# A sixth buffer of split weights and a fourth of raw weights, in room taken from the dynamic DMA scratch

## The chip, the cores and the metric

The kernel runs on one core of a Trainium2 chip, as one launch. The metric is the device time of that launch in microseconds, as the median of several runs. The engines are TensorE (PE in the profile; PEld its weight loads), VectorE (DVE), ScalarE (ACT), GpSimd (POOL) and SyncE (SP), each with an instruction stream of its own.

## The reference, cut to what matters

One inference step of a small backbone of two trunk layers, in fp32, over 640 tokens (512 latent tokens of a 2-D grid and 128 context tokens) of 1024 channels:

```
every layer: x += 1/2 * gate1 * SwiGLU1(mod(rmsnorm(x)))
             x += gate2 * Mixer_l(mod(rmsnorm(x)))
             x += 1/2 * gate3 * SwiGLU2(mod(rmsnorm(x)))
layer 0:     Mixer = w_in -> [2-D neighbourhood attention | bidirectional RG-LRU] -> w_out_ab
layer 1:     Mixer = real part of the 2-D DFT of the normalised input, then w_out_c
mod(h)     = h * (1 + scale) + shift;  shift, scale, gate from SiLU(cond) @ w_ada[l] + b_ada[l]
swiglu(h)  = (silu(h @ w_gate) * (h @ w_up)) @ w_down
```

So there are four FFNs, two mixers, and the products for the modulation vectors (w_ada). Outputs are the tokens, new context keys and values, and the last states of the RG-LRU.

## The kernel before

**Layout.** x is kept transposed (channels on partitions), as two halves of 320 tokens. A product in fp32 is made of three passes of a shorter format: with each operand split into a high and a low part, it adds high·high, high·low and low·high (`mm3`, L271).

**Weights.** They come from HBM as *units* of 128x1024 numbers. SP issues the load (`load`, L129) into a *raw* buffer (tile `st`, 4 KB of each partition). ACT makes the high part (`whi`, L176), and DVE the low part (`wlo`, L181, subtracting the high part from the raw weights), into a *pair* (`whi` and `wlo` together, 8 KB of each partition). In the program `split_later` (L174) emits ACT's instruction and leaves DVE's to `flush` (L179), which comes at the head of the next `prep`. During the attention POOL makes the low parts.

The kernel has 3 raw buffers and 5 pairs for its whole length (L51). A phase adds its own: each FFN adds 3 raw buffers, the attention 1 pair and 4 raw buffers, and the opening 5 raw buffers.

**The order of the work** is written out by the Python program: each engine runs its instructions in the order in which they were emitted, and the semaphores between the engines are put in from the tiles used. `prep(upto, most)` (L151) is called between the matmuls. It emits the next steps of weight preparation, in a fixed list, as long as their item's number lies under `upto`, a raw buffer has been filled by a load, and a pair is free. Then `load` issues the loads for which raw buffers are free. `done()` frees the oldest unit's pair and calls `prep(n_use + LS)`, with LS = 4 units ahead of the one in use. So the number of buffers and the two limits together decide at which place of DVE's and ACT's streams a split is put.

**FFN.** The inner width is cut into chunks. The first two take 4 units (gate and up of two chunks), which run chunk by chunk while the norm of the input is made (`mm_side`, L285, `ffn_body`, L726; the first FFN of all has `ffn_start`). Beside them runs the norm of half 1, `norm_steps`, whose first three steps are emitted together (`step(3)`, after the fifth of the eight chunks of half 0). Ahead of them come the sums `nst`, the reciprocal root on DVE (a chain of eleven instructions on 128x3 numbers, `nv`, `ns` and `nt`, L415 to L422) and the factors `dg`, which PE spreads over the partitions (`nbc`, L453). The chunks after that are *quads*: gate and up of a chunk, each in two halves, form a 2x2 matrix, for which the Strassen–Winograd scheme needs 7 products in place of 8. A quad has two raw units and makes three pairs from them: `A1`, `S24` and `S3` (plus a single-part buffer, `S1`). Its steps are `quad_a` (split of A1), `quad_b` and `quad_c` (two sums each on POOL, L226 to L232, in place in the raw buffers), `quad_f` (split of S24), `quad_d` (split of S1, tile `s`) and `quad_e` (split of S3, which frees the second raw buffer). `quad_c` overwrites the raw unit that `A1` was split from, and so it waits for that `wlo`; the split of S24 reads what `quad_c` makes. In a quad the products are matmuls into `q`; the products of the first two chunks go to `pg`, and those with w_down to `pd`.

**In time** (from the profile): FFN 1 of layer 0 is 0 to 500 us, mixer 0 is 500 to 838 (attention about 690 to 778), then FFN 2 of layer 0 to 1300, FFN 1 of layer 1 to 1745, the Fourier mixer to 1850, and FFN 2 of layer 1 to the end. Text and rows call the last three of the FFNs' beginnings the second, third and fourth *entry*.

**Small loads.** Two constants, `pk` (192 KB) and `pk2` (27 KB), hold the biases and the norm's weights. POOL issues their loads at the start (L1619, L1621); they are the only transfers on its queue. All weights are loaded by SP.

Of the kernel before, what the change touches and what calls it, by code (L numbers as in the profile page):

```python
# [13 lines left out]
PSUM = bass.MemoryType.PSUM  # L14
# [18 lines left out]
class Item:  # L33
    """weights of one product: their loads, the steps that split them, what the steps made"""
# [7 lines left out]
class Kern:  # L42
    def __init__(self, ctx, nc, tc, a):
        self.ctx, self.nc, self.tc, self.a = ctx, nc, tc, a
        pool = lambda name, bufs, **k: ctx.enter_context(tc.tile_pool(name=name, bufs=bufs, **k))
        self.const = pool("const", 1)
        self.t2 = pool("t2", 2)
        self.ps2 = pool("ps2", 2, space=PSUM)
        self.ps_st, self.ps_pairs = ctx.enter_context(ExitStack()), None
        self.st_free, self.w_free = [], []  # L50
        self.buffers(self.const, None, 3, 5)  # L51
        self.loads, self.steps, self.items, self.used = [], [], [], []
        self.n_use = 0
        self.LS = 4
        self.limit = 9999
        self.lows, self.b12, self.t_todo, self.nst = [], {}, [], {}
        self.add_eng = None
        self.T_ENG = [nc.gpsimd if x == "p" else nc.vector for x in TE]
        self.s_dma = self.s_use = 0
        self.slab_t = {}  # L60
        self.ada_m = None
        self.low = nc.vector

    def buffers(self, pool, phase, n_st, n_w):
        """buffers for weights: as loaded, and split; those of a phase serve its weights only"""
        for j in range(n_st):
            self.st_free.append((pool.tile([P, 1024], F32, name=f"st{j}"), phase))
        for j in range(n_w):
            self.w_free.append((pool.tile([P, 1024], F32R, name=f"whi{j}"),
                                pool.tile([P, 1024], F32R, name=f"wlo{j}"), phase))  # L70
# [14 lines left out]
    def slab_pool(self, st, upto, bufs=2):  # L85
        """weights of the adaLN vectors: slabs up to this one are used in the phase"""
        self.slab_p = st.enter_context(self.tc.tile_pool(name="slab", bufs=bufs))
        self.s_dma = self.s_use
        self.s_end, self.s_bufs = upto, bufs

    def psum(self, pairs):
        """PSUM of a phase: six single banks or three pairs"""
        if self.ps_pairs is pairs:
            return
        self.ps_st.close()
        self.ps_pairs = pairs
        ps = self.ps_st.enter_context(self.tc.tile_pool(name="ps", bufs=3 if pairs else 6, space=PSUM))
        if pairs:
            self.pair = lambda name: ps.tile([P, 2, 512], F32, tag="mm", name=name)
            self.bank = lambda name: self.pair(name)[:, 0, :]  # L100
        else:
            self.bank = lambda name: ps.tile([P, 512], F32, tag="mm", name=name)
# [48 lines left out]
    def prep(self, upto, most=99):  # L151
        """steps for the items up to this one, as far as there are buffers"""
# [21 lines left out]
    def split_later(self, it, hi, lo, src, then=None):  # L174
        """the low part comes with the next step"""
# [20 lines left out]
    def fold_a(self, it, w):  # L196
        """rows m and -m: sum and difference"""
# [12 lines left out]
    # a pair of units as a 2 x 2 matrix (unit, half of the rows): the seven left factors of Strassen and Winograd  # L210
# [59 lines left out]
    def done(self, most=99):  # L270
        """the oldest unit in use is no longer needed"""  # L271
        self.free_slot(self.used.pop(0), 0)
        self.prep(self.n_use + self.LS, most)

    def mm3(self, out, w, ks, xs, first=True, last=True):
        """out (+)= W^T X in three passes; w: (hi, lo) as [P, k, 128], xs: k -> (hi, lo)"""
# [8 lines left out]
    def mm_side(self, outs, ws, h, lag=0):  # L285
        """products of several units with half h, chunk after chunk as the norm gives them; the last two unit by unit
        lag: chunks by which the last unit stays behind"""
# [57 lines left out]
    def ada_end(self):  # L345
        """the finished vector, channels on partitions"""
# [28 lines left out]
    def parts(self, h):  # L375
        """pieces of a token half with one condition: (column slice, condition)"""
# [20 lines left out]
    def norm_s(self, h, bank=None):  # L397
        """sums of squares, tokens on partitions"""
# [6 lines left out]
    def norm_a(self, h):  # L405
        """rsqrt(mean(x^2) + eps)"""
# [4 lines left out]
    def rsqrt(self, ps, n=3):  # L411
        """rsqrt(mean(x^2) + eps) of n columns of sums"""
# [3 lines left out]
        # the exponent halved on the bits, then Newton's steps  # L416
# [21 lines left out]
    def T_pool(self, ks=range(4)):  # L438
        """right factors of Strassen and Winograd beside the parts of h"""
# [9 lines left out]
    def norm_r(self):  # L449
        """the factors of the tokens on all partitions"""  # L450
# [6 lines left out]
    def norm_high(self, h, l, i, c, r, keep):  # L457
        """h = rms_norm(x) g (1 + scale) + shift and its high part
        keep: for the products of a SwiGLU"""
# [24 lines left out]
    def direct(self, l, i, h, c, keep):  # L484
        """the high part comes without the sum of product and shift"""
# [19 lines left out]
    def norm_steps(self, h, l, i, keep=False):  # L505
        """a step for each chunk, low parts one step behind"""
# [17 lines left out]
    def t_sums(self, k, b12, b22):  # L524
        """T1 = B12 - B11, T2 = B22 - T1, T3 = B22 - B12, T4 = B21 - T2"""
# [21 lines left out]
    # slabs of a SwiGLU: after chunks of the first units, and after each quad  # L547
# [5 lines left out]
    def plan_ffn(self, l, n, s):  # L553
        """weights of a SwiGLU in the order of their use; s: the first slab, returns the next"""
# [36 lines left out]
    def ffn(self, l, i, after, mid=iter(()), late=None):  # L591
        """after(h, c): what follows the last update of chunk c, half h; mid: steps of other work, one in each quad;
        late: what follows the last quad"""
# [14 lines left out]
    def ffn_start(self, evac):  # L608
        """the first products of all: the first two vectors of adaLN come chunk by chunk, the norm and the products follow"""
# [7 lines left out]
        def ada(c):  # L617
            """the vectors' values for a chunk, four sums in groups of columns"""
# [178 lines left out]
    def down_last(self, fs, gate, after):  # L797
        """the last product before a norm: half 0 is through while four chunks of half 1 remain
        the first sums wait for the last chunk of the inner width"""
# [20 lines left out]
    def quad(self, f, fills, begin=False):  # L820
        """gate and up of a chunk, both halves of the tokens, in seven products
        M1 = A11 B11, M2 = A12 B21, M3 = S4 B22, M4 = A22 T4, M5 = S1 T1, M6 = S2 T2, M7 = S3 T3;
        C11 = M1 + M2, U2 = M1 + M6, C12 = U2 + M5 + M3, C21 = U2 + M7 + M4, C22 = U2 + M7 + M5"""
# [73 lines left out]
    def out_last(self, xs, gate, after):  # L897
        """the last product before a norm: half 0 is through while four chunks of half 1 remain"""
# [32 lines left out]
    def mix_setup(self):  # L931
        """parameters of the mixer, log_sigmoid(lambda)"""
# [13 lines left out]
        # y = |lam|, w = exp(-y) by halving steps and a series  # L946
# [17 lines left out]
        # log1p(w) = 2 artanh(w / (2 + w))  # L964
# [11 lines left out]
        # -2 log_sigmoid = 2 (2 artanh) - 2 min(lam, 0)  # L976
# [24 lines left out]
    def lru(self, c, xc, gel):  # L1001
# [21 lines left out]
        for d in range(2):  # L1023
            # exp(-z) and t = tanh(z / 2): 1 - a = t (1 + a), 1 - a^2 = t (1 + a)^2
# [28 lines left out]
    def qk_norm(self, which, c, ps):  # L1053
        """RMS norm over each head's 64 channels; q also gets -1/8"""
# [47 lines left out]
    def mixer0(self, after):  # L1102
        nc, tc = self.nc, self.tc
        self.bg, self.fg = [], []
        with ExitStack() as st:
# [18 lines left out]
            with ExitStack() as s2:  # L1124
# [60 lines left out]
                def early():  # L1185
                    """work that the first tiles of the attention cover"""
# [41 lines left out]
    def bias(self, c, v):  # L1228
        """mask less position bias of a variant of the windows' columns"""
# [122 lines left out]
    def fourier_const(self):  # L1352
        """the DFT matrices in the place of the right factors, a step for each piece"""
# [18 lines left out]
        def steps():  # L1372
# [9 lines left out]
            # the shift times the root of the number of tokens, by chunk in the group, group, condition  # L1382
# [10 lines left out]
    def scaled(self, h, c):  # L1393
        """x g (1 + scale) in parts; the factors of the tokens follow the channels' transform"""
# [12 lines left out]
    def fourier_front(self, const):  # L1407
        """what follows the updates before the transform"""
# [25 lines left out]
    def tok_rest(self):  # L1434
        """factors of the other tokens; the third tile has the end of half 0 and the start of half 1"""
# [8 lines left out]
    def fourier(self, after):  # L1444
        nc, tc = self.nc, self.tc
        NP, NQ, MP, MQ = self.NP, self.NQ, self.MP, self.MQ
        with ExitStack() as st:
# [6 lines left out]
            with ExitStack() as s2:  # L1454
# [11 lines left out]
                def chan(k, g):  # L1466
                    """the channels' transform: token tile k, group g"""
# [9 lines left out]
                def chan_out(k, g):  # L1477
                    """times the factors of the tokens, in parts"""
# [26 lines left out]
                # the shift's part, the same for all tokens  # L1505
# [25 lines left out]
                def pos(r):  # L1531
                    """rows r: cosines of group r, 4 the Nyquist channels, 5 + g sines of group g"""
# [9 lines left out]
                    def shift(q):  # L1542
                        """the shift stays at the first position"""
# [18 lines left out]
            with ExitStack() as s2:  # L1562
# [14 lines left out]
                for c in range(KD):  # L1577
# [17 lines left out]
                    # token n has the sum, the one as far from the end the difference  # L1595
# [16 lines left out]
    def run(self, stop=99):  # L1612
        nc, a = self.nc, self.a
        const = self.const
        with self.tc.manual_schedule():
# [3 lines left out]
            nc.gpsimd.dma_start(out=pk, in_=a["pk"])  # L1619
            self.pk2 = const.tile([P, 54], F32, name="pk2")  # L1620
            nc.gpsimd.dma_start(out=self.pk2, in_=a["pk2"])  # L1621
# [48 lines left out]
            def after(l, i, first=4, per=3, keep=True):  # L1670
                """the next norm: half 0 while the last products of half 1 run"""
# [49 lines left out]
def pack(inp):  # L1721
    """lays the inputs out; no arithmetic"""
# [9 lines left out]
    # the first two vectors by chunks of channels  # L1732
# [47 lines left out]
    # DFT matrices: channels (columns: cosines 0..127, the first halved, cosine 128, sines 1..127) and positions  # L1780
# [37 lines left out]
```

## Time and profile before

| | |
|---|---|
| device time, three runs | 2305.51, 2307.77, 2308.82 us (median 2307.77) |
| span of the profiled execution | 2305.0 us |
| instructions | 39901 |
| PE busy | 2224.0 us (96%), 15534 matmuls |
| DVE, ACT, POOL busy | 1554.8, 990.7, 954.9 us |
| HBM | 245.44 MB moved, 105 GB/s |

The span runs from the first to the last instruction of one execution, and is the profiled execution's own time; no other time is given for it. A timeline row gives the start and the duration of an instruction (or of several alike in a row, "x2"), what it writes and reads, and in brackets how long its engine had been idle and which instruction, of which engine and line, ended that. "us" in the table of stretches is busy time per engine, and the number between 0 and 1 after the engines is TensorE's granted clock as a share of 2.4 GHz.

### The profile page before, as it was taken

The page shows a single profiled execution, that of the slowest core. Times are in us where ns is not written, and L with a number is a line of the kernel's source. Part 1 is how long each engine was busy: PE and PEld are TensorE (multiplying, and loading weights), DVE is VectorE, ACT ScalarE, POOL GpSimd, SP SyncE. Part 2 cuts the span into 40 slices and gives each one's busy share as a digit, 9 for nine tenths or more (in the row PEclk, how much of TensorE's full clock was granted, in tenths as well). Part 3 has the DMA queues.
Part 4 walks back from the last instruction along what each step waited for, and adds up shares of the span by engine and source line. Part 5 has one row for each costly group of instructions (what it writes and reads, how often), then busy time and mean ns, then how long its engine had stood idle before and what let it go on. Part 6 is the DMA issues. An engine that isn't in the chain of part 4 may idle for free.

```text
span 2305.0 us, 39901 instructions
## 1 busy us (share of the span) xinstructions
PE 2224.0 (96%) x15534; PEld 2110.0 (92%) x15534; DVE 1554.8 (67%) x2871; ACT 990.7 (43%) x1780; POOL 954.9 (41%) x856
## 2 busy tenths in 40 slices
PE   7999999999998899999999999999999989999999
PEld 5889999999994788999999889999999979999999
DVE  6676677666865368666666786666667786666665
ACT  4433333347855435333333453333335553333332
POOL 2444444440023235444444454444443645444441
PEclk9999999999999999999999999999999999999999
DMA  7333333321228424333322243332332322222221
GB/s 278 113 111 105 105 107 107 115 74 56 73 71 267 131 83 137 110 101 110 106 91 97 75 155 120 110 97 96 103 117 62 128 85 83 83 83 83 83 89 57
DMA packets 75316, 245.44 MB, mean 106 GB/s; under 512 B 8756, under 2 KB 12996, under 8 KB 75128
## 3 DMA queue, kind: packets, MB, share of 16 engines
q1 hardware_dynamic: 74168, 241.28, 31.7%
q8 instruction: 123, 2.02, 0.4%
q10 hardware_dynamic: 864, 1.38, 0.2%
q14 instruction: 65, 0.53, 0.1%
q0 software_dynamic: 96, 0.22, 0.0%
HBM read 239.71 MB, written 3.15 MB: 105 GB/s over the span
## 4 chain that ended last, share of the span: by engine, by line
PE 79%; DVE 13%; ACT 4%; issue 2%; POOL 2%; DMA 1%; ACTq 0%; DVEq 0%; SPq 0%; POOLq 0%
PE q L282 40%; PE pd L282 26%; PE pj L282 5%; DVE wlo L181 2%; PE ada L327 2%; DVE tl L172 1%; PE pg L282 1%; PE gt L1014 1%; PE pos L1549 1%; DVE x L381 1%; PE S L1262 1%; DVE y L473 1%; DVE sx L1268 1%; PE PT L1288 1%; DMA st<-w_ada 1%
## 5 line engine op out<-in xcount | busy, mean ns | idle before, releaser
L181 DVE TENSOR_TENSOR wlo<-st,whi 128x1024 fp32r<-128x1024 f32 (+2 forms) x401 | 498.4, 1254 | 11.1 <-ACT whi L176 10.2
L176 ACT ACTIVATE whi<-st 128x1024 fp32r<-128x1024 f32 (+2 forms) x405 | 401.2, 992 | 233.0 <-POOL st L232 139.3
L282 PE MATMUL pd<-g,whi 128*128 128x320 f32 x1536 | 347.0, 310 | 4.3 <-DVE u L825 2.3
L381 DVE SCALAR_TENSOR_TENSOR x<-pd,mods,x 128x128 f32<-128x128 f32 (+2 forms) x696 | 265.0, 433 | 111.7 <-PE pd L282 111.2
L282 PE MATMUL q<-hh,wlo 128*128 128x320 f32 x960 | 296.9, 309 | 5.3 <-DVE wlo L181 5.3
L282 PE MATMUL q<-hh,whi 128*128 128x320 f32 x960 | 300.7, 313 | 1.0 <-DVE u L825 1.0
L282 PE MATMUL q<-th,whi 128*128 128x320 f32 x960 | 297.3, 310 | 3.0 <-DVE sg L825 3.0
L282 PE MATMUL q<-tl,whi 128*128 128x320 f32 x960 | 296.6, 309 | 0.7 <-POOL tl L172 0.7
L282 PE MATMUL q<-th,wlo 128*128 128x320 f32 x960 | 296.6, 309 | 0.0
L282 PE MATMUL q<-hl,whi 128*128 128x320 f32 x960 | 296.3, 309 | 0.0
L231 POOL TENSOR_TENSOR st<-sums,st 128x512 f32<-128x512 f32 x80 | 118.0, 1474 | 396.9 <-DVE wlo L181 359.5
L825 POOL TENSOR_TENSOR u<-u,u 128x320 f32<-128x320 f32 x80 | 106.5, 1331 | 401.0 <-DVE u L825 401.0
L282 PEld LDWEIGHTS pd<-g,whi 128*128 128x128 f32 x1536 | 256.8, 188 | 8.9 <-DVE x L381 3.1
L282 PE MATMUL pd<-hh,whi 128*128 128x320 f32 x768 | 238.4, 310 | 0.0
L282 PE MATMUL pd<-hl,whi 128*128 128x320 f32 x768 | 237.9, 310 | 0.0
L282 PE MATMUL pd<-g,wlo 128*128 128x320 f32 x768 | 237.7, 310 | 0.0
L282 PE MATMUL pd<-hh,wlo 128*128 128x320 f32 x768 | 236.8, 308 | 0.0
L826 ACT ACTIVATE sg<-sg 128x320 f32<-128x320 f32 x160 | 75.4, 471 | 284.5 <-DVE sg L825 284.5
L282 PEld LDWEIGHTS q<-hh,whi 128*128 128x128 f32 x960 | 180.2, 188 | 16.8 <-issue 8.6
L282 PEld LDWEIGHTS q<-th,whi 128*128 128x128 f32 x960 | 180.3, 188 | 6.6 <-issue 4.7
L282 PEld LDWEIGHTS q<-hh,wlo 128*128 128x128 f32 x960 | 180.2, 188 | 6.4 <-DVE wlo L181 6.4
L282 PEld LDWEIGHTS q<-tl,whi 128*128 128x128 f32 x960 | 180.4, 188 | 1.5 <-POOL tl L172 1.5
(327 smaller groups left out, 5016.0 us busy)
## 6 DMA issues: line engine op xcount, KB each, us to landing
st<-w_ada SPq DMA_DIRECT2D x144, 512.0 KB, 4.6
st<-ffn_gate SPq DMA_DIRECT2D x88, 512.0 KB, 3.6
st<-ffn_up SPq DMA_DIRECT2D x88, 512.0 KB, 3.7
st<-ffn_down SPq DMA_DIRECT2D x96, 384.0 KB, 3.1
st<-w_in SPq DMA_DIRECT2D x20, 512.0 KB, 3.5
st<-ffn_down SPq DMA_DIRECT2D x16, 512.0 KB, 3.5
st<-w_out_ab SPq DMA_DIRECT2D x8, 512.0 KB, 3.5
st<-w_out_c SPq DMA_DIRECT2D x8, 512.0 KB, 3.5
```

Of the source, the lines that this page charges most:

```text
L172: (eng or self.nc.vector).tensor_tensor(out=lo, in0=src, in1=hi.bitcast(F32), op=ALU.subtract)
L176: self.nc.scalar.activation(out=hi, in_=src, func=AF.Copy)
L181: self.low.tensor_tensor(out=lo, in0=src, in1=hi.bitcast(F32), op=ALU.subtract)
L231: self.nc.gpsimd.tensor_tensor(out=s[:, 0:512], in0=it.s1, in1=s[:, 0:512], op=ALU.subtract)
L282: self.nc.tensor.matmul(out, lhsT=l, rhs=r, start=first and j == 0, stop=last and j == len(ops) - 1)
L327: nc.tensor.matmul(self.ada_ps[32 * j:32 * j + 32, 0:256], lhsT=self.s_sb[:, k, :], rhs=t[:, 256 * j:256 * j + 256], start=k == 0, stop=k ...
L381: self.nc.vector.scalar_tensor_tensor(out=self.x[h][c][:, sl], in0=ps[:, sl], scalar=gate[:, c, r:r + 1], in1=self.x[h][c][:, sl], op0=ALU ...
L473: nc.vector.tensor_tensor(out=y, in0=self.x[h][c], in1=r, op=ALU.mult)
L825: tt = lambda e, o, a, b, op=ALU.add: e.tensor_tensor(out=o, in0=a, in1=b, op=op)
L826: cp = lambda o, p, fn=AF.Copy: nc.scalar.activation(out=o, in_=p, func=fn)
L1014: nc.tensor.matmul(g[:, s, 0:322], lhsT=wt[:, d, j, :], rhs=xc[:, 322 * s:322 * s + 322], start=True, stop=True)
L1262: nc.tensor.matmul(o, lhsT=q, rhs=k, start=True, stop=True)
```

## The change

The pool of dynamic DMA scratch of the program is set to 1024 bytes. The two small loads are issued by ScalarE, in front of its first activation, in place of GpSimd. In the room, `buffers` gets 4 raw buffers and 6 pairs in place of 3 and 5 for the kernel's whole length: 4 KB and 8 KB of each partition. No limit of `prep` and no order of steps is changed. The other lines of the diff take out comments and docstrings and leave the line numbers as they were.

```
@@ Kern.__init__ @@
-        self.buffers(self.const, None, 3, 5)
+        self.buffers(self.const, None, 4, 6)
...
@@ Kern.run @@
-            nc.gpsimd.dma_start(out=pk, in_=a["pk"])
+            nc.scalar.dma_start(out=pk, in_=a["pk"])
             self.pk2 = const.tile([P, 54], F32, name="pk2")
-            nc.gpsimd.dma_start(out=self.pk2, in_=a["pk2"])
+            nc.scalar.dma_start(out=self.pk2, in_=a["pk2"])
...
@@ kernel @@
-    nc = _bacc.Bacc("TRN2", target_bir_lowering=False, num_devices=1)
+    nc = _bacc.Bacc("TRN2", target_bir_lowering=False, num_devices=1, dynamic_dma_scratch_size=1024)
```

## Rows read from the trace of the kernel before

**Rows 1.** The page: busy us of each engine (share) x instructions.

```profile
PE 2224.0 (96%) x15534; PEld 2110.0 (92%) x15534; DVE 1554.8 (67%) x2871; ACT 990.7 (43%) x1780; POOL 954.9 (41%) x856
```

**Rows 2.** Stretches: start:end, length, busy us by engine, granted clock, DMA share, GB/s.

```profile
510.00:520.00 10.00, 7.45 (x45) 7.22 (x43) 7.97 (x17) 5.60 (x11) 7.87 (x26) 0.83 0.28 98
850.00:860.00 10.00, 7.48 (x30) 7.17 (x31) 6.35 (x18) 3.47 (x7) 3.12 (x4) 0.66 0.22 84
1100.00:1150.00 50.00, 50.00 (x349) 48.79 (x348) 32.98 (x56) 18.14 (x30) 21.56 (x16) 1.00 0.29 95
1310.00:1320.00 10.00, 5.85 (x39) 5.27 (x37) 9.08 (x17) 1.27 (x2) 5.33 (x5) 1.00 0.51 181
```

**Rows 3.** Waits of PE: us in all, times, longest.

```profile
PE q L282 <- DVE wlo L181: 5.3, 4, 1.7
```

**Rows 4.** Timeline of PE, 838 to 906: start, duration, instruction, [idle before <-releaser].

```profile
852.52 1.81 PE L453 MATMUL nbc<-dg,ones 128*128 128x128 f32 x6 [3.44 <-DVE dg L430]
...
854.69 0.47 PE L282 MATMUL pg<-hl,whi 128*128 128x320 f32 x1
...
861.88 0.31 PE L282 MATMUL pg<-hh,whi 128*128 128x320 f32 x1
...
887.96 0.42 PE L282 MATMUL q<-hh,wlo 128*128 128x320 f32 x1 [1.64 <-DVE wlo L181]
```

**Rows 5.** Timeline of DVE, 838 to 890.

```profile
843.88 2.35 DVE L181 TENSOR_TENSOR wlo<-st,whi 128x1024 fp32r<-128x1024 f32 x2
...
846.34 1.07 DVE L417 TENSOR_SCALAR ns<-nv 128x3 int32<-128x3 int32 x1
...
854.36 0.49 DVE L473 TENSOR_TENSOR b<-x,nbc 128x320 f32<-128x320 f32 x1 [1.51 <-PE nbc L453]
...
861.24 0.49 DVE L729 TENSOR_TENSOR sg<-sg,pg 128x320 f32<-128x320 f32 x1 [3.03 <-ACT sg L728]
```

**Rows 6.** Timeline of POOL, 838 to 862.

```profile
845.28 2.11 POOL L226 TENSOR_TENSOR sums<-st 128x512 f32<-128x512 f32 x1 [1.66 <-DMA st<-ffn_up]
```

**Rows 7.** Timeline of PE, DVE and POOL, 1308 to 1322.

```profile
1313.96 0.42 PE L282 MATMUL pg<-hh,wlo 128*128 128x320 f32 x1 [2.62 <-DVE wlo L181]
...
1311.63 3.41 DVE L181 TENSOR_TENSOR wlo<-st,whi 128x1024 fp32r<-128x1024 f32 x2
...
1320.53 0.49 DVE L473 TENSOR_TENSOR b<-x,nbc 128x320 f32<-128x320 f32 x1 [0.68 <-PE nbc L453]
...
1315.18 1.29 POOL L231 TENSOR_TENSOR st<-sums,st 128x512 f32<-128x512 f32 x1 [2.36 <-DVE nv L415]
```

**Rows 8.** Timeline of DVE and POOL, 1850 to 1892.

```profile
1866.33 1.23 DVE L181 TENSOR_TENSOR wlo<-st,whi 128x1024 fp32r<-128x1024 f32 x1
1867.47 0.48 DVE L473 TENSOR_TENSOR b<-x,nbc 128x320 f32<-128x320 f32 x1
...
1867.70 1.29 POOL L231 TENSOR_TENSOR st<-sums,st 128x512 f32<-128x512 f32 x1 [3.60 <-DVE wlo L181]
```

**Rows 9.** Timeline of PE and SP, 752 to 772.

```profile
756.02 0.64 PE L327 MATMUL ada<-st,s_sb 128*32 128x256 f32 x8
...
757.44 0.64 PE L327 MATMUL ada<-st,s_sb 128*32 128x256 f32 x8
...
769.92 0.98 PE L1288 MATMUL PT<-ident,sx 128*128 128x128 f32 x6 [3.58 <-DVE sx L1279]
...
758.14 4.46 SPq L139 DMA_DIRECT2D st<-w_out_ab  x3
```

**Rows 10.** Timeline of ACT, DVE and PE from the start; one DMA issue of ACT.

```profile
2.56 1.28 ACT L1641 ACT_TABLE_LOAD   x1 [2.56 <-DMA cT<-cT]
...
16.79 0.16 DVE L637 TENSOR_TENSOR mods<-ada,pk 128x4 f32<-128x4 f32 x1
...
120.17 0.56 PE L282 MATMUL pd<-g,whi 128*128 128x320 f32 x2 [2.26 <-DVE u L825]
...
1748.11 0.38 ACTq L1370 DMA_DIRECT2D cst<-ch  x1
```

## The prediction

> **What bounds the kernel now.** First the page's busy times: PE is busy for 2224.0 of 2305.0 us, so all that a change of buffers can win is 81 us of idle time, and no matmul is added or removed [rows 1]. Then the table of stretches: in a steady stretch of quads (1100 to 1150) PE is busy for 50.00 of 50 us at clock 1.00, with DVE at 32.98 and POOL at 21.56 [rows 2]. There no wait is left for a buffer to remove. The idle time sits at the changes of phase: 1310 to 1320 has 5.85 us of PE, 850 to 860 has 7.48 us at clock 0.66, 510 to 520 has 7.45 us at 0.83 [rows 2]. Then PE's waits, to see which of them name the preparation of weights: its quads waited for `wlo` four times in 2305 us, 5.3 us in all [rows 3]. Last the timelines of the entries, where one sees that the waits for `wlo` and for the norm of half 1 are one queue: DVE does the low parts and the root, in the order of emission [rows 4 to 8]. So the sum is made entry by entry.
>
> **Part 1: the two small loads.** They go in front of ScalarE's first operation. ScalarE waits until 2.56 us there for another load (`cT`), and one DMA issue on its queue took 0.38 us [rows 10]; two are 0.8 us, under that wait. The data are read first at 16.79 us, by DVE [rows 10]. I take 0; bounds −0.3 (POOL's masks come sooner, no wait of the rows names them) and +0.8 (both issues in full ahead of the first activation, if `cT` came at once). The small scratch itself costs nothing that I can find: nothing else used POOL's queue.
>
> **Part 2: steady quads, w_down, projections.** 0, since PE covers all. The limits of `prep` (units ahead of the one in use) aren't raised, so a pair more is mostly a pair that lies free. If the cover went, one `wlo` of 1.23 us [rows 8] per quad would be 80 x 1.23 = 98 us; DVE's 33 of 50 us say that it won't. Bounds −0.5 and +1.
>
> **Part 3: the first FFN.** A split comes a step earlier: one wait of PE for DVE's `u` at 120.17, of 2.26 us, is shortened by what DVE no longer does in front of it [rows 10]. I take −0.4, nearest to the small wait changes; bounds −2.3 (all of it) and +1.9 (a `wlo` of 1.23 and an `s` of about 0.7, half as wide, now put ahead of the sums for the right factors).
>
> **Part 4: into the mixer and out of the attention.** At 510 to 520 the splits ahead of PE's wait stay the same in number, because a low part is emitted with the next step: 0, bounds −1.2 and +1.2 (one `wlo` fewer or more). At the attention's end the first load of `w_out_ab` is issued at 758.14, once the slab read by PE at 757.44 has set a raw buffer free; with a fourth it can go one slab earlier, after 756.02 [rows 9]. That is 1.4 us, and the splits behind it crowd less into the softmax that PE waits 3.58 us for at 769.92 [rows 9]. I take −1.4; bounds −2.0 and 0 (the wait is for `sx`, whose own work stays).
>
> **Part 5: the second entry.** Before the norm of half 1, DVE runs two `wlo` in a row (2.35 us from 843.88), then the root from 846.15, whose small steps take 1.07 us at times [rows 5] while POOL makes `quad_b` and `quad_c` from 845.28, started by the landing of a load [rows 6]. PE waits 3.44 us for the end of it, and then its matmuls run at the half clock: from 854.69 to 861.88 there are 35 of them in 7.19 us, where 349 in 50 us would make 5.0 [rows 2, 4]. A sixth pair and fourth raw buffer let one of the two `wlo` go a step earlier (−1.2) and the load land sooner, so that less of POOL lies over the root (−0.8): −2.0. The quad's wait for the S24 split, 1.64 us at 887.96 [rows 4], goes too: the split is emitted ahead of the norm's chunks, its `wlo` in DVE's gap of 1.51 us at 854.36 and its `s` in that of 3.03 us at 861.24 [rows 5]: −1.6. Together −3.6; bounds −4.5 and −1.0 (only the quad's wait, less some of it).
>
> The Trainium skill, SBUF — State Buffer, "Who interferes with whom", says that a DVE instruction with two SBUF inputs is blocked for the whole length of a GpSimd instruction that reads SBUF, and the other way round. The trace agrees: the root step at 846.34, on 128x3 numbers, took 1.07 us while POOL ran [rows 5, 6]. By the rule, a split moved onto POOL's sums buys less than its length; rival A is what that gives.
>
> **Part 6: the third entry.** Here the two `wlo` are 3.41 us, PE waits 2.62 us for the first, and `quad_c` is at 1315.18, beside the root [rows 7]. One `wlo` fewer in front is −1.7, the quad's later wait −1.7 (the longest of the four [rows 3]); the S24 `wlo` no longer has a gap (0.68 us at 1320.53 [rows 7], against 1.23): +0.5. Sum −2.9; bounds −3.4 and +1.0 (the waits merge into one long enough for the clock to fall; after 2.62 us it stayed at 1.00, while at 510 to 520, with 2.55 us of idle PE, it is 0.83 [rows 2, 7]).
>
> **Part 7: the fourth entry.** Here the pair does harm. The norm of half 1 starts on DVE at 1867.47, right behind the `wlo` of A1, which ends at 1867.56; POOL's `quad_c` waits for that same `wlo`, starts at 1867.70 and takes two operations of 1.29 us [rows 8], so it ends at about 1870.4. Before, the S24 split had no pair and came later. Now it is emitted ahead of the norm's first steps, and both ACT's high part and DVE's low part stand at the head of their queues and wait for `quad_c`: 1870.4 + 1.0 + 1.23 = 1872.6, so 5.1 us later for the norm. PE needs its chunks soon after. Back come the quad's wait of 1.6 and the `wlo` of 1.23 that DVE has done by then: 5.1 − 1.6 − 1.2 = +2.3. Bounds −1.6 (the split stays behind the norm, only the wait goes) and +3.5 (only the wait comes back).
>
> **Sum.** 0 + 0 − 0.4 − 1.4 − 3.6 − 2.9 + 2.3 = −6.0 us, against the profiled 2305.0 us. The profiled execution is 2.8 us under the median of the runs, 2307.8; I put the sum on the median: 2301.8.
>
> **Rivals.**
> A. *DVE gives it back.* What leaves PE's waits at the entries returns in the norm, since DVE has 9.08 busy of 10 us at 1310 to 1320 [rows 2] and the same number of splits must still run beside the same norm. For: gaps of 0.68 us. Against: the second entry has gaps of 1.51 and 3.03. Gains of parts 5 and 6 shrink to the attention's 1.4 and one wait of 1.6, less 2.3 at the fourth, −0.7: about 2307.
> B. *The buffers aren't used where PE waits.* `prep`'s limits bind, not the buffers, and raw buffers are plentiful within an FFN. For: the steady stretch has no wait for them [rows 2]. Against: at each entry four of the five pairs are held. 0 to −0.5: 2307.5.
> C. *Slower.* The split that waits for `quad_c` is put ahead of the norm not at the fourth entry alone, but at the second and third too. It decides from the point where POOL's `quad_c` ends later than the norm's factors are there; in the third it ends at about 1315.18 + 2 x 1.29 = 1317.8, and DVE's norm begins at 1320.53 [rows 7], so there are 2.7 us to spare, about two `wlo`. Price about 2.0 at each of these (the fourth's 2.3, with more to spare), 3.5 at the fourth, less 1.8 from attention and start: +5.7, 2313.5.
> D. *The half clock goes too.* A shorter wait at 852.52 spares the 2.2 us of slow matmuls, and that at 769.92 perhaps 1.7 (the clock's loss of 0.17 over 10 us): −6.0 − 3.9 = −9.9, about 2297.9.
>
> The Trainium skill, TensorE: Matmul & The Clock Gate, Part 1, says that the array falls back to 1.2 GHz after idling. The row with clock 0.66 agrees for a wait of 3.44 us, but 2.62 us at 1313.96 left it at 1.00, so the trace doesn't say which waits are long enough; D rests on that.
>
> **How the numbers follow.** Forecast 0.45 (own range 2298 to 2305), A 0.17, B 0.10, C 0.16, D 0.12. The range goes from just below D to inside C, 2296 to 2311, and leaves out some 2 in 10. A measurement tells 0.2%, 4.6 us, from no change: faster means under 2303.2, slower over 2312.4. D and three quarters of the forecast are faster: 0.12 + 0.34 = 0.46, and a little of A makes 0.48. Two thirds of C and the unforeseen are slower: 0.15. The rest, 0.37, is the same.
>
> **What would show it.** At the second entry one `wlo` between `hl` and `nv`, and a wait at `nbc` near 1.4 us. At the third, the same with no wait for `wlo` of 1.7 at the first quad. At the fourth, ACT's `whi` right before the first `y` and behind POOL's `quad_c`, and the norm 3 to 5 us later. At the attention, `w_out_ab` issued 1.4 us earlier. In steady stretches, 50.00 of 50 still. I am wrong if the waits at the entries keep their length (B), if they only move to `nbc` or `hl` (A), or if PE waits for a split behind `quad_c` in the second and third entries (C).

## The result: slower by some 0.6%

The changed kernel takes 2320.98 us (median of 5; 2315.51 to 2321.23) against 2305.51 us (2302.19 to 2308.82): a ratio of 1.0059, with a 95% interval of 1.0048 to 1.0070. Built and run once more it took 2322.03 us, ratio 1.0066 (1.0054 to 1.0079). The forecast was 2301.8, and the range ended at 2311.

The page of the changed kernel has the same matmuls and more idle time: the span is 2319.4 us, of which PE is busy for 2231.2, so 88 us are idle in place of 81 [rows 1], and PE's busy time itself grew by 7 with the same matmuls: the mean granted clock is 0.988 in place of 0.992. DVE and POOL are busy longer with the same work, by 55 and 68 us.

```profile
PE 2231.2 (96%) x15534; PEld 2116.1 (91%) x15534; DVE 1610.1 (69%) x2871; ACT 983.9 (42%) x1780; POOL 1022.7 (44%) x854
```

The table of stretches answers to [rows 2]; the events lie some us earlier or later here than in the kernel before. The steady stretch has 50.00 of 50 us still, as forecast; 510 to 520 and 850 to 860 have less idle PE, but clocks of 0.83 and 0.68; 1310 to 1320 now has 0.86. A new stretch of idling and half clock is at 1355 to 1365.

```profile
510.00:520.00 10.00, 9.50 (x55) 9.23 (x56) 5.35 (x24) 2.41 (x5) 4.30 (x23) 0.83 0.20 76
850.00:860.00 10.00, 10.00 (x50) 9.66 (x50) 6.48 (x13) 5.46 (x10) 2.13 (x2) 0.68 0.16 54
1100.00:1150.00 50.00, 50.00 (x349) 48.79 (x348) 34.28 (x52) 17.17 (x29) 25.25 (x18) 1.00 0.30 97
1310.00:1320.00 10.00, 6.55 (x36) 5.94 (x35) 9.45 (x20) 2.29 (x4) 4.02 (x4) 0.86 0.15 54
1355.00:1365.00 10.00, 8.40 (x34) 6.82 (x35) 5.08 (x8) 4.49 (x9) 4.96 (x5) 0.50 0.17 60
```

PE's waits show what took the place of those in [rows 3]: no quad waits for `wlo` any more, but the first quad of each of the three entries waits for `tl`, the low part of a right factor, once for one made by DVE and once for one made by POOL, both from the sums of the activations. In the kernel before, PE waited for DVE's `tl` nowhere, for POOL's 0.7 us and for `nbc` 7.8 us.

```profile
PE q L282 <- DVE tl L172: 10.8, 3, 4.0
PE nbc L453 <- DVE dg L430: 10.7, 7, 3.5
...
PE q L282 <- POOL tl L172: 3.0, 3, 2.0
```

**Where the time goes.** The two programs have the same matmuls in the same order, so the start of one matmul in one trace, less its start in the other, is the delay there. The table gives how much that delay grows in each stretch (us; landmarks are matmuls of the kernel before at these times; a minus is time won; stretches left out change by less than 1.3). "Again" is the second build; the columns of the experiments are read below.

| stretch of before | changed | again | e1 | e2 | e3 | e4 | e6 | e7 | e8 | e9 | e10 |
|---|---|---|---|---|---|---|---|---|---|---|---|
| 0–480, first FFN | −4.1 | −3.3 | −3.3 | −2.6 | −1.5 | −2.4 | +1.3 | −2.2 | −1.3 | −2.3 | −0.2 |
| 480–778, mixer and attention | +2.2 | +3.6 | +3.4 | +5.1 | +3.6 | +0.5 | +0.9 | +0.7 | +5.6 | +3.2 | +1.3 |
| 778–886, second entry, norm | −1.0 | 0.0 | −2.5 | −3.2 | +1.3 | −3.2 | −2.5 | −2.3 | −3.2 | +3.1 | −4.9 |
| 886–950, second entry, quad | +1.4 | +1.4 | −0.9 | +1.9 | +2.1 | −0.8 | +1.4 | −0.5 | −0.8 | −1.7 | −0.1 |
| 1309–1412, third entry | +6.0 | +5.4 | −0.2 | +3.9 | +6.7 | −0.2 | +5.1 | 0.0 | −0.3 | +3.5 | −2.7 |
| 1779–1846, Fourier mixer | +5.2 | +5.2 | +5.2 | +0.5 | +5.3 | +0.5 | +5.3 | 0.0 | +5.2 | +0.5 | 0.0 |
| 1846–1945, fourth entry | +4.8 | +4.5 | +2.3 | +6.7 | +3.5 | +2.9 | +4.4 | −0.1 | +2.3 | +3.1 | +0.5 |
| sum up to 1945 | +14.1 | +16.5 | +3.7 | +12.1 | +20.7 | −3.2 | +15.6 | −3.1 | +7.1 | +9.0 | −5.6 |

These are single profiled executions: that of the changed kernel was the slowest of its five runs, and those of e2, e4, e7 and e9 were the fastest of theirs. Up to the Fourier mixer, changed, again and e2 have the same instructions, and yet their first three rows differ by 1.5 to 3.2 us, that of the third entry by 2.1, and that of the second entry's quad by 0.5. Changed and again differ by 0.3 in the last row. Less than that is not read from one row.

**The third entry.** In the kernel before, POOL made the last right factor at 1354.10 to 1357.0, and then the sums of the *second* quad (1356.98). The timeline of POOL in the kernel before:

```profile
1349.33 0.88 POOL L528 TENSOR_TENSOR b<-b,hl 128x320 f32<-128x320 f32 x1 [0.83 <-DVE b L528]
1354.10 1.01 POOL L528 TENSOR_TENSOR t<-hh,y 128x320 f32<-128x320 f32 x1 [3.89 <-DVE y L528]
...
1356.15 0.88 POOL L172 TENSOR_TENSOR tl<-t,th 128x320 fp32r<-128x320 f32 x1
1356.98 1.53 POOL L226 TENSOR_TENSOR sums<-st 128x512 f32<-128x512 f32 x1
```

In the changed kernel the four sums of the second quad stand ahead of it. They start at 1349.24, the third waits 2.36 us for a `wlo`, and the last factor's first operation (`t<-hh,y`) comes at 1357.22. On DVE two `wlo`, of S3 and of the second quad's A1, stand ahead of the splits that the quad needs. Beside POOL's sums they take 3.44 us, where two in a row took 2.35 in [rows 5], and the `tl` behind them take 1.55 and 1.56. PE waits 3.96 us for the second of these, then 0.42 for POOL's factor, and runs at the half clock afterwards (0.50 in 1355 to 1365). The rows of POOL, DVE and PE:

```profile
1349.24 1.30 POOL L226 TENSOR_TENSOR sums<-st 128x512 f32<-128x512 f32 x1
1350.62 1.42 POOL L227 TENSOR_TENSOR st<-st,st 128x512 f32<-128x512 f32 x1
1354.40 1.38 POOL L231 TENSOR_TENSOR st<-sums,st 128x512 f32<-128x512 f32 x1 [2.36 <-DVE wlo L181]
1355.86 1.41 POOL L232 TENSOR_TENSOR st<-st 128x512 f32<-128x512 f32 x1
1357.22 1.12 POOL L528 TENSOR_TENSOR t<-hh,y 128x320 f32<-128x320 f32 x1
...
1350.82 3.44 DVE L181 TENSOR_TENSOR wlo<-st,whi 128x1024 fp32r<-128x1024 f32 x2
...
1354.58 1.55 DVE L172 TENSOR_TENSOR tl<-b,th 128x320 fp32r<-128x320 f32 x1
1356.05 1.56 DVE L172 TENSOR_TENSOR tl<-y,th 128x320 fp32r<-128x320 f32 x1
...
1356.18 0.64 PE L282 MATMUL q<-tl,s 128*128 128x320 f32 x1 [3.96 <-DVE tl L172]
...
1360.17 0.63 PE L282 MATMUL q<-tl,whi 128*128 128x320 f32 x1 [0.42 <-POOL tl L172]
```

How they got there: with a sixth pair the split of S24 and that of S1 are emitted while half 0 is still multiplied. So the steps that are emitted while half 1 is (one at each unit set free) are no longer these, but the next ones of the fixed list: S3, then the second quad's A1, `quad_b` and `quad_c`. Waits of the same kind stand at the second entry (3.96 and 0.60 us, the first ending at 890.24) and at the fourth (2.90 and 1.96).

**The norms at the entries.** At the second, one `wlo` stands ahead of the root in place of two, and the S24 `wlo` (849.93) comes behind the factors, beside PE's `nbc`. But POOL's sums still lie over the root (1.07 us at 844.35), and PE waits for `nbc` nearly as long as in [rows 4]. In the second build, with the same instructions, that wait is 1.70 us. At the third entry PE waits 3.45 us for `nbc`, and no longer 2.62 for `wlo` ahead of it. Rows of PE and DVE, answering to [rows 4, 5]:

```profile
849.56 1.81 PE L453 MATMUL nbc<-dg,ones 128*128 128x128 f32 x6 [3.21 <-DVE dg L430]
...
842.16 2.08 DVE L181 TENSOR_TENSOR wlo<-st,whi 128x1024 fp32r<-128x1024 f32 x1
...
844.35 1.07 DVE L417 TENSOR_SCALAR ns<-nv 128x3 int32<-128x3 int32 x1
...
849.93 1.23 DVE L181 TENSOR_TENSOR wlo<-st,whi 128x1024 fp32r<-128x1024 f32 x1
```

At the fourth, ACT's `whi` of S24 waits for POOL's `quad_c`, DVE's `wlo` for ACT, and the norm of half 1 starts at 1880.29. With the delay of 7.7 us that the trace has by then, that is 1880.3 − 1867.5 − 7.7 = 5.1 us late. Rows of POOL, ACT and DVE, answering to [rows 8]:

```profile
1875.37 1.28 POOL L231 TENSOR_TENSOR st<-sums,st 128x512 f32<-128x512 f32 x1 [3.59 <-DVE wlo L181]
1876.73 1.29 POOL L232 TENSOR_TENSOR st<-st 128x512 f32<-128x512 f32 x1
...
1878.06 1.06 ACT L176 ACTIVATE whi<-st 128x1024 fp32r<-128x1024 f32 x1 [8.47 <-POOL st L232]
...
1879.15 1.23 DVE L181 TENSOR_TENSOR wlo<-st,whi 128x1024 fp32r<-128x1024 f32 x1 [3.92 <-ACT whi L176]
1880.29 0.48 DVE L473 TENSOR_TENSOR b<-x,nbc 128x320 f32<-128x320 f32 x1
```

**The Fourier mixer**, of which the prediction says nothing. One more unit of w_out_c is folded ahead of the first output product: two more sums on POOL and two more low parts on DVE lie ahead of the split of the last Fourier results. PE waits 0.74 us for their `hh` and 0.61 for their `hl`, and runs at the half clock behind. Rows of POOL and PE, then the stretch 1817 to 1822, with a clock of 0.69:

```profile
1816.58 1.27 POOL L201 TENSOR_TENSOR sums<-st 128x512 f32<-128x512 f32 x1 [0.63 <-DVE wlo L172]
...
1817.00 0.42 PE L1588 MATMUL yp<-hh,whi 128*128 128x324 f32 x1 [0.74 <-ACT hh L171]
...
1818.86 0.63 PE L1588 MATMUL yp<-hl,whi 128*128 128x324 f32 x1 [0.61 <-DVE hl L172]
```

```profile
1817.00:1822.00 5.00, 4.27 (x13) 3.09 (x14) 3.23 (x8) 1.13 (x4) 4.51 (x7) 0.69 1.02 404
```

### The profile page after: what moved, and what is told of

Same layout as the page of the kernel before. It is cut to its first block, busy times and chain, and to the rows that moved or that the text cites. A ratio compares the mean times of both kernels' runs of the same rounds, so it can differ in the third digit from the quotient of the medians.

```text
span 2319.4 us, 39836 instructions
## 1 busy us (share of the span) xinstructions
PE 2231.2 (96%) x15534; PEld 2116.1 (91%) x15534; DVE 1610.1 (69%) x2871; ACT 983.9 (42%) x1780; POOL 1022.7 (44%) x854
## 5 line engine op out<-in xcount | busy, mean ns | idle before, releaser
L181 DVE TENSOR_TENSOR wlo<-st,whi 128x1024 fp32r<-128x1024 f32 (+2 forms) x401 | 515.9, 1298 | 46.9 <-ACT whi L176 46.1
L176 ACT ACTIVATE whi<-st 128x1024 fp32r<-128x1024 f32 (+2 forms) x405 | 393.0, 992 | 167.6 <-POOL st L232 160.8
L825 POOL TENSOR_TENSOR u<-u,u 128x320 f32<-128x320 f32 x80 | 98.2, 1228 | 510.5 <-DVE u L825 262.1
L381 DVE SCALAR_TENSOR_TENSOR x<-pd,mods,x 128x128 f32<-128x128 f32 (+2 forms) x696 | 258.2, 430 | 88.6 <-PE pd L282 88.4
L231 POOL TENSOR_TENSOR st<-sums,st 128x512 f32<-128x512 f32 x80 | 139.3, 1742 | 256.3 <-DVE wlo L181 253.0
L282 PEld LDWEIGHTS q<-th,wlo 128*128 128x128 f32 x960 | 182.5, 190 | 0.0
L282 PEld LDWEIGHTS q<-hl,whi 128*128 128x128 f32 x960 | 180.8, 188 | 0.0
```

What stands on the lines that cost most here:

```text
L176: self.nc.scalar.activation(out=hi, in_=src, func=AF.Copy)
L181: self.low.tensor_tensor(out=lo, in0=src, in1=hi.bitcast(F32), op=ALU.subtract)
L231: self.nc.gpsimd.tensor_tensor(out=s[:, 0:512], in0=it.s1, in1=s[:, 0:512], op=ALU.subtract)
L282: self.nc.tensor.matmul(out, lhsT=l, rhs=r, start=first and j == 0, stop=last and j == len(ops) - 1)
L381: self.nc.vector.scalar_tensor_tensor(out=self.x[h][c][:, sl], in0=ps[:, sl], scalar=gate[:, c, r:r + 1], in1=self.x[h][c][:, sl], op0=ALU ...
L825: tt = lambda e, o, a, b, op=ALU.add: e.tensor_tensor(out=o, in0=a, in1=b, op=op)
```

## Experiments

All ran in five rounds beside the kernel before, which had medians of 2305.9 to 2307.0 us there.

**e1, the next quad's steps held.** In `ffn_body`, on the changed kernel:

```
                     if (n, j, h) == (EQ, 3, 1):
                         self.quad(2, 0, True)
+                        self.limit = self.n_use
                     if (n, j, h) == (6, 3, 1):
                         step(9)
                         self.t_end()
+                        self.limit = 9999
```

> The changed kernel, with one thing more: at the second to fourth entries the steps of the quad after the first quad wait until the last right factor of the first quad has been made (an index limit that is lifted after it). My theory: in the changed kernel these steps (two low parts on DVE, four sums on POOL) now stand ahead of the last right factors, and PE waits 4.0, 4.0 and 2.9 us for them; with the limit these waits go, and 10 to 14 us of the 14 that were lost come back: 2307 to 2311 against 2321. The rival: the steps have to be done on DVE and POOL anyway, so the wait only moves into the next quad: 2317 to 2321.

2312.91 us, ratio 1.0028 (1.0018 to 1.0038): 7 to 9 us of the 14 to 16 are gone, a little less than the 10 that I had put at the least. The waits of 3 to 4 us for `tl` are gone (0.4 us is left at each entry), POOL makes the last factor at 1349.52 and the sums behind it, and the rows of the second, third and fourth entry shrink by 2.3, 6.2 and 2.5 us. Nothing of it returns later. The rival falls. On DVE, at the third entry, only S3's `wlo` is left ahead of the quad's splits, and it takes 1.22 us. Rows of POOL:

```profile
1349.52 1.01 POOL L528 TENSOR_TENSOR t<-hh,y 128x320 f32<-128x320 f32 x1 [2.15 <-DVE y L528]
...
1351.57 0.86 POOL L172 TENSOR_TENSOR tl<-t,th 128x320 fp32r<-128x320 f32 x1
1352.40 1.53 POOL L226 TENSOR_TENSOR sums<-st 128x512 f32<-128x512 f32 x1
```

**e2, the sixth fold held.** On the changed kernel, `self.limit = 9999` ahead of the Fourier products becomes:

```
+                self.limit = self.n_fold + 5
...
+                    self.limit = 9999
                     self.done()
```

> The changed kernel, with one thing more: in the Fourier mixer the sixth w_out_c unit is folded only after the first output product, as with one pair fewer. My theory: its fold (two sums on POOL, two low parts on DVE) stands ahead of the split of the Fourier result, for which PE waits 0.7 and 0.6 us and then runs at the lower clock; that is 3.5 to 5 us: 2316 to 2318. The rival: the delay there is POOL's and DVE's own, whatever the order: 2321.

2321.66 us, ratio 1.0067 (1.0054 to 1.0079): no faster, so this expectation failed. The time is the rival's, but its reason isn't what the trace shows. In the trace the waits are gone, the clock stays at 1.00 (the stretch 1817 to 1822 below), and the Fourier row falls from +5.2 to +0.5. But the next row rises from +4.8 to +6.7: part of the delay had been made up behind the Fourier mixer in any case. What remains, 2.8 us in the trace, is not seen in the times, whose intervals reach 3 us to either side.

```profile
1817.00:1822.00 5.00, 5.00 (x33) 4.61 (x32) 2.49 (x6) 1.04 (x2) 4.49 (x7) 1.00 0.99 359
```

**e3, the S24 split held** until the first norm steps are out, at all three entries. In `prep`, and set in `ffn_body` around the first half:

```
             it, fn, need = self.steps[0]
+            if self.hold_f and fn == self.quad_f:
+                return
...
                         elif n == 4:
                             step(3)
+                            self.hold_f = False
```

> The changed kernel, with one thing more: at the second to fourth entries the split of S24 waits until the first norm steps of half 1 have been emitted. The step of my prediction for the fourth entry says that this split, ahead of the norm, waits for POOL's second pair of sums and holds the norm up: 3 us come back there. At the second and third entries it cost nothing, and 1.6 us of waiting may come back at each. So 2317 if only the fourth counts, 2321 if all three do; the rival, that the norm is late for another reason: 2321 to 2324, with no change at the fourth entry.

2326.22 us, ratio 1.0083 (1.0071 to 1.0095), so it is not faster, and perhaps slower than the changed kernel (the intervals overlap); none of the times that I had given came. The fourth row falls by 1.0 to 1.3, the rows of the second and third entry rise by 0.7 to 2.3, which is hardly more than executions of one kernel differ there. So the split ahead of the norm is worth about 1.2 us of loss at the fourth entry, and no gain from holding it shows at the others.

**e4, all three** (S24 at the fourth entry only).

> The three together, the split of S24 held at the fourth entry only. If the three theories hold and add up: 2321 - 12 - 4 - 3 = 2302, a little faster than the kernel before, since the first FFN gained 4.1 us in the trace and keeps that. If the lost time only moves: 2312 or more.

2309.11 us, ratio 1.0009 (1.0000 to 1.0017). So 12 to 13 us of the 14 to 16 come back, between the two answers given. Two of the three holds bring nothing alone (e2, e3), but together they bring 3.8 us on top of e1. The trace is 3.2 us under the kernel before, the times are not.

**e5, the loads and the scratch alone** (3 raw buffers, 5 pairs).

> Only the small scratch and the two loads on ScalarE's queue; 3 raw buffers and 5 pairs as before. My theory: nothing, 2305 to 2308, with waits at the entries as in the kernel before. The rival: the loads or the scratch change the opening, and the 4.1 us that the changed kernel gained in the first FFN are here too: 2301 to 2304.

2307.71 us, ratio 1.0003 (0.9994 to 1.0011): nothing.

**e6 and e7, one kind of buffer each:** `self.buffers(self.const, None, 3, 6)` and `(self.const, None, 4, 5)`.

> The changed kernel with 3 raw buffers and 6 pairs. My theory: the sixth pair is what lets the next quad's steps, the S24 split and the sixth fold run ahead, so the loss is here in full: 2317 to 2322, with waits of some 4 us for the last right factors at the entries and the 5 us in the Fourier mixer. The rival: the steps run ahead because the raw weights are there sooner, which needs the fourth raw buffer: 2304 to 2309.

> The changed kernel with 4 raw buffers and 5 pairs. My theory: no harm at the entries, since five pairs hold the steps back as before; loads come sooner, by 1 to 4 us in all: 2303 to 2307. The rival, by which the raw buffer does it: 2315 to 2321.

The sixth pair alone: 2323.89 us, ratio 1.0069 (1.0055 to 1.0082), all of the loss, and 2 us above the range that I gave. The fourth raw buffer alone: 2307.16 us, ratio 1.0001 (0.9992 to 1.0010), nothing. Their waits show it, first with six pairs, then with five, where PE waits for `wlo` as in [rows 3]:

```profile
PE q L282 <- DVE tl L172: 11.9, 3, 4.0
```

```profile
PE q L282 <- DVE wlo L181: 5.6, 4, 1.6
```

In the first FFN every kernel with four raw buffers gains 1.3 to 4.1 us in its trace, and those with three change by −0.9 (e5, not in the table) to +1.3. That is the one gain of the fourth raw buffer in all its traces, and it is too small for the times.

**e8, only POOL's sums of the next quad held**, as in e1 but by `if it.idx >= self.lim_b and fn == self.quad_b: return` in `prep`.

> The changed kernel; at the second to fourth entries only the next quad's two pairs of sums on POOL (and what follows them) wait for the last right factor, while the split of its first pair (one high part on ACT, one low part on DVE) may run ahead. If the four sums on POOL, 5.4 us at least, ahead of the last right factor's own POOL work are the cause: the waits of 4 us go, 2309 to 2314, as with all steps held. If DVE's low parts are: the waits stay at 3 us or more, 2317 to 2321. If each does a part: between.

2313.63 us, ratio 1.0030 (1.0019 to 1.0041), as e1. At the third entry two waits of 0.6 us are left, one for DVE and one for POOL, in place of 3.96 and 0.42. POOL makes the last factor first, then the sums. The two `wlo` stand ahead on DVE as in the changed kernel, so the four sums on POOL are what PE waited for. The rows show two ways in which they did it: POOL's own last factor came behind them, and DVE was slower beside them. Without them DVE's two `wlo` take 2.35 us in place of 3.44, and the two `tl` 0.48 and 0.95 in place of 1.55 and 1.56; it was the second `tl` that ended PE's wait of 3.96 us. What each of the two ways costs by itself was not tried. Rows of POOL, DVE and PE:

```profile
1354.07 0.99 POOL L530 TENSOR_TENSOR t<-hh,y 128x320 f32<-128x320 f32 x1 [3.28 <-DVE y L530]
...
1356.93 1.52 POOL L228 TENSOR_TENSOR sums<-st 128x512 f32<-128x512 f32 x1
...
1351.17 2.35 DVE L183 TENSOR_TENSOR wlo<-st,whi 128x1024 fp32r<-128x1024 f32 x2
...
1353.84 0.48 DVE L174 TENSOR_TENSOR tl<-b,th 128x320 fp32r<-128x320 f32 x1
1354.46 0.95 DVE L174 TENSOR_TENSOR tl<-y,th 128x320 fp32r<-128x320 f32 x1
...
1354.38 0.42 PE L284 MATMUL q<-tl,s 128*128 128x320 f32 x1 [0.64 <-DVE tl L174]
...
1357.02 0.41 PE L284 MATMUL q<-tl,whi 128*128 128x320 f32 x1 [0.61 <-POOL tl L174]
```

**e9 and e10, the first quad's sums held until the norm's first steps are out**: in `prep`, `if self.hold_b and fn == self.quad_b: return`, lifted behind `step(3)`. e9 is the changed kernel with this and the holds of e1 and e2; e10 the kernel before with this alone.

> The changed kernel with the next quad's steps held until the last right factor, the sixth fold held, and at the second to fourth entries the first quad's sums on POOL held until the first norm steps of half 1 are emitted. In the kernel with all three holds PE still waited 3.3 us for the norm's factors at the third entry and 1.7 at the second, while DVE's root steps took over 1 us beside POOL's sums. If the sums beside the root are the cause, these waits shrink by 3 to 5 us in all, and so does the 4 us before the fourth entry's norm: 2302 to 2306, under the kernel before. The rival: the sums then run beside the norm of half 1 and its right factors, where DVE and POOL have no room, and PE waits there: 2307 to 2312.

> The kernel before (3 raw buffers, 5 pairs, loads on POOL) with that last hold alone. If the overlap of POOL's sums with the root is worth something without the new buffers: 1 to 4 us less, 2303 to 2306. With five pairs the S24 split comes late anyway, so the quad's wait of 1.6 us at each entry stays; if the sums then delay it further: 2308 to 2312.

e10 took 2303.58 us, ratio 0.9990 (0.9980 to 1.0000): the lowest of all, at the edge of what can be told from no change. The waits for `nbc` fall to 2.9 us in four, with 0.8 the longest (before: 3.44 at one place, [rows 4]), and the rows of the second and third entry are −4.9 and −2.7. The hold is not alone in this: in e7, without it, no wait for `nbc` is over 0.9 either, and the second entry gains 2.3, the third nothing; e5, with the instructions of the kernel before there, gains 1.5 at the second. So the hold's own gain is seen at the third entry only. e9 took 2319.68 us, ratio 1.0049 (1.0036 to 1.0062). There PE waited twice for a load of w_ada, 15.5 us in all: SP issues the loads in order, raw buffers came free late, and nine issues for w_ada at the second entry stretch over 36 us. Of the two answers given neither was this. The waits of e10 for `nbc`, then those of e9 for loads:

```profile
PE nbc L455 <- DVE dg L432: 2.9, 4, 0.8
```

```profile
PE ada L329 <- DMA st<-w_ada: 15.5, 2, 7.9
```

**e11, e10's hold with four raw buffers and five pairs.**

> The changed kernel with 4 raw buffers and 5 pairs, and the first quad's sums on POOL held until the first norm steps of half 1 are emitted. The hold alone gave 2303.6 on the old buffers, the fourth raw buffer alone 2307. In the kernel with six pairs and this hold PE waited 7.6 us for a load of w_ada at the third entry, since raw buffers came free late. If a fourth raw buffer helps against that: 2301 to 2304. If it is worth nothing: 2303 to 2306. If loads wait here too: 2308 or more.

2305.72 us, ratio 0.9996 (0.9988 to 1.0005): nothing beyond e10, the middle answer. The second entry's row is −2.1, as in e7 without the hold (−2.3); the third's is −1.8, against 0.0.

**e12, the changed kernel again.**

> The changed kernel once more, to see how far the time of one and the same kernel moves between builds and loads: the kernels with one hold each differ from it by 1 to 8 us. If it comes to 2319 to 2323 again, the 8 us of the held next quad are real, and so are the 5 us by which the held S24 split was slower; if it comes to 2325, the latter are not.

2322.03 us. So the two builds of this kernel lie within about 1 us, and the 8 us of e1 are real. By the rule that I had set, e3's excess of 4 us would be real too; I leave it open, since the intervals of the ratios overlap.

No kernel with the sixth pair beat the one before.

## Why the prediction was wrong

**The step that failed** stands in part 2 and is used in 5 to 7: "The limits of `prep` (units ahead of the one in use) aren't raised, so a pair more is mostly a pair that lies free." Pairs, not limits, held the steps back: with five, the list stopped at the S24 split until the first of the four units was done; with six, the four steps that come as the four units are set free reach two steps further at each entry, to `quad_b` and `quad_c` of the next quad. For steady quads the step of part 2 held (50.00 of 50 us); at the entries it did not. Parts 5 to 7 moved S24 forward and left what follows it in the list where it was. But the list is one queue, and the steps behind moved too: a `wlo` and four sums of a quad that isn't needed yet, ahead of the right factors that were. The prediction saw POOL's sums stretch DVE's work beside them at the root, and did not ask what other sums would come to lie beside. e1 and e8 price this at 7 to 9 us in time, 11 in e1's trace (2.3 + 6.2 + 2.5). It is the largest term, and the sum has no entry for it.

**The second missing term** is the Fourier mixer: the same mechanism, with a sixth fold. 5.2 us in its own row, of which 2 are made up right after; alone it doesn't show in the times (e2), and with e3's hold at the fourth entry it is worth 3.8 us on top of e1 (e4).

**Part 1**, 0: right as far as the times tell (e5).

**Part 3**, −0.4, bounds −2.3 to +1.9: −4.1 and −3.3 in the traces, from the fourth raw buffer. The wait at 120.17 went as a whole. The clock at 40 to 60 and 60 to 80 was 0.83 and 0.85 before; it stayed at 1.00 in the changed kernel, but was 0.83 and 0.91 in the second build, so it is not what won the time. Mis-sized and outside the bounds, in the right direction.

**Part 4**, 0 into the mixer: the delay changes by −0.2 and 0.0 us from 480 to 515 (changed and again). −1.4 at the attention: the load of `w_out_ab` went out at 754.54 for 758.14, of which 2.2 us is the lead that the trace had by then and 1.4 the slab, as forecast. But PE's wait of 3.58 us for `sx` only broke up (2.26 us at 762.67 and 1.28 at 770.27 are the longest), and the stretch ends at +2.2. As it varies between +0.5 and +5.6 among kernels with the same instructions there, no gain or loss is shown.

**Parts 5 and 6**, −3.6 and −2.9. The wait for S24's `wlo` went, as said, and one `wlo` left the place ahead of the root. Of the −2.0 and −1.7 ahead of `nbc`, about 1 came at the third entry, where waits of 2.62 and 1.53 us became one of 3.45: the root still runs beside POOL's sums, which is rival A's mechanism. At the second entry it isn't settled: the wait for `nbc` is 3.21, 1.70 and 1.70 us in changed, again and e2, against a forecast of 1.4, and the row −1.0, 0.0 and −3.2. How much the sums over the root cost is seen at the third entry, where taking them out of the way wins 2.7 us on the old buffers (e10) and 1.8 with the fourth raw buffer (e11 against e7). In e9's trace, with POOL idle at the third entry, every root step is 0.15 to 0.17 us long; beside the sums some take 1.07 to 1.15. The Trainium skill, SBUF — State Buffer, "Who interferes with whom", says that DVE and GpSimd shut each other out where DVE reads two SBUF inputs; the trace agrees for the steps of two inputs (up to 1.15 us). The step at 846.34, which the prediction put under that rule [rows 5], has one, so for it the rule was misapplied; the same section also names DVE's two-port modes, and no run here tells whether this was one.

**Part 7**, +2.3: the mechanism is shown, down to the 5.1 us by which the norm is late; its worth, by e3, is about 1.2 (by e4, with the changes of this row in e1 and e2 taken off, 1.3), inside the bounds.

**The rivals.** C had the right side, with under half of the price (+5.7 against 15) and the wrong place: the splits ahead of the norm at the second and third entries do wait for `quad_c` without harm, as the 2.7 us to spare had said. B and D fell: the buffers were used, and the half clock came back at new places. D's 1.7 us at 769.92 were read from the row 510 to 520; the stretch 760 to 780 itself has 0.91 in the kernel before, 1.8 us over its 20.

## What to carry to other kernels

A buffer more in an in-order schedule moves not one step but all that stand behind it in the list; follow the list to the point where it stops again, and ask what is queued behind the last step that it now reaches. Work that is off the critical path may be early only on an engine that has nothing due: hold it by its due time, not by whether a buffer is free. Ask of the engine beside it too: here the sums on POOL also stretched DVE's steps. When a count of buffers has served as the brake, put an explicit limit in its place before raising it.

## Not expected of the hardware

The same instructions took different times in single executions: from 480 to 778 us between 0.5 and 5.6 us longer than in the kernel before, and at the second and third entry up to 3 and 2 us apart in changed, again and e2. Part of it is the clock. At the third entry PE waits 3.45, 3.45 and 3.46 us for `nbc` in these three, and in the 7 us behind the wait the granted clock is 0.76, 0.51 and 0.76. In the kernel before, 2.62 us of waiting at 1313.96 [rows 7] left it at 1.00, and 2.55 us of idle PE at 510 to 520 did not (0.83) [rows 2]. In the Fourier mixer of the changed kernel the half clock came after waits of no more than 0.74 and 0.61 us (0.69 at 1817 to 1822). Why the attention varies most was not tried.
